# Side work of the mixers emitted by an account of engine times instead of at fixed distances

## The chip, the cores and the metric

One core of one Trainium2 chip runs the whole program. The metric is the device time of that core in microseconds (us), the median of several runs. Five instruction streams matter: TensorE (PE, matrix multiplications and transposes), VectorE (DVE), ScalarE (ACT), GpSimd (POOL) and SyncE (SP, which issues the DMAs). Each engine runs its own instructions in the order in which the program lists them; an instruction whose operand is not there holds back everything behind it on its engine.

## The reference, cut to what matters

Two layers run over 1024 prompt positions and 8 samples of 4 positions, 1056 columns in all, of width 1024.

```python
def _trunk(x, ...):
    for layer in range(DEPTH):                 # 2 layers
        h = _rmsnorm(x, p['norm_mix'][layer])
        if layer % 2 == 0:
            y, ... = _ab_mixer(h, ...)         # S5 scan + retention, 4 heads
        else:
            y, st = _hgrn_mixer(h, ...)        # gated recurrence, 8 heads
        x = x + y
        h = _rmsnorm(x, p['norm_ffn'][layer])
        y, buf = _conv_ffn(h, ...)             # gate, conv, silu, up, down
        x = x + y
    return _rmsnorm(x, p['norm_final']), ...
```

A mixer is a dense projection (`h @ w_in`), a recurrence over positions for each head, a norm of each head's output, a gate, and a dense projection back. All is in float32.

## The kernel before

**Dense work.** Every dense projection is cut into tiles of 128 output rows, and each tile into three column chunks of 384, 384 and 288 (`CH`). A float32 product is made of three reduced-precision ones (`mm1`: high with high, high with low, low with high), so a chunk of a mixer tile is 8 x 3 = 24 matmuls on line 258, into one of four PSUM buffers `acc`. After a chunk, `evac` moves it out, mostly with a DVE instruction (line 673 for the S5 input, 1032 to 1034 for rotated q and k, 1046 for v, 1460 for the q of layer 1).

**Jobs and ticks.** `run_jobs` (line 221 on) takes the tiles in a fixed list. After each k step `mm` advances a clock, `self.now`, by 1/8, so one chunk is one **tick** and one tile is three. `at(dt, fn)` files a piece of side work under a due time in ticks; `tick` runs what is due, and what runs is placed at that point in the program order of every engine that it uses. `chain` files a series of steps with given distances. All distances are constants in the table `P`. Nothing looks at whether the operands of a due step will be there: if not, PE, being in order, stands still. `flush` runs all that is left.

**Layer 0** (`layer0`, line 418 on). Input tiles u0 to u3, then for each of 4 heads the tiles q, k and v, then four gate tiles; before the last gate tile, `open2` flushes. Side work: the S5 scan, as `s5_x` (per unit u of 8, two pairs: `pair` builds operands on DVE and POOL, `turn` transposes on PE at line 856, `prod` multiplies at line 865), then `s5_within` (28 calls of five DVE instructions, lines 880 to 884), `s5_samples`, `s5_carry` (15 calls of the same five), then `s5_y` (per unit two pairs: spread, `toep` at line 971, `prod` at line 987). Beside it the retention of each head: `first(n)` (score and transpose, lines 1145 and 1146; `kt` copied by ACT at line 1150) and `second(n)` (lines 1161 to 1164; the state `S` is updated by DVE at line 1169), eight times, a sample chain `sample0` to `sample3`, and `head_norm` (line 1212 on).

**Layer 1** (`layer1`, line 1407 on). For each of 8 heads the tiles q, f and v; from the sixth head on a gate tile follows each head (`LAG` = 5), so the first five heads are 9 ticks long and the others 12. Side work is filed by `hgrn` at the end of the f tile: for each of three chunks `prep`, `scans` (1566, 1567), `base` (1578 to 1584), `level` three times (1601 to 1609) and `kfin` (1613); eight times `first(nn)` (1652, 1653, `levels` 1636, a masked DVE copy of the scores at 1657, `kt` copied by ACT at 1659) and `second(nn)` (1670 to 1673, the state `S` at 1676 or 1678 by DVE); the sample chain; and `head_norm`: `square`, `mean` (line 334, on `nl` made by POOL at line 325), `newton`, and `scale` (line 1235), once for each chunk.

With the constants of `P` (span 9, so u = 0.75 ticks), counted from the start of a nine-tick head: `first(n)` is due at 9.8 + 0.75 n, `second(n)` 1.05 later, the last step of the sample chain at 17.0, the head norm begins at 17.1, its three `mean` steps are due at 18.1, 18.5 and 18.8 and the first `scale` at 19.7. The q tile of the head after next begins at tick 18.

Of the kernel before, what the change touches and what calls it, by code (L numbers as in the profile page):

```python
# [11 lines left out]
F32R = mybir.dt.float32r  # L12
# [31 lines left out]
P = {"uP": 25, "qrV": 4, "loA": 3, "spV": 2, "wi": 0, "en2": 0, "stats": 1.281, "prep": 0.508, "fin": 0.8, "n1A": 1.101, "n1C": 1.0, "n2A": 0.386, "n2C": 0.45, "n3A": 0.501, "n3C": 0.375, "n4A": 0.558, "n4C": 0.78, "nsA": 0.429, "nsC": 0.339,   # L44
# [31 lines left out]

class Trunk:
    def __init__(self, ctx, tc, I, O):
        self.tc, self.nc, self.I, self.O = tc, tc.nc, I, O
        nc = self.core = self.nc  # L80
# [5 lines left out]
        self.uid = 0  # L86
        self.held = set()
# [106 lines left out]
    def at(self, dt, fn):  # L194
        self.seq += 1
        self.side.append(((self.now if self.base is None else self.base) + dt, self.seq, fn))
        self.side.sort(key=lambda x: x[:2])
# [5 lines left out]
    def put(self, dst, src, dt=None):  # L203

        self.at(P["put"] if dt is None else dt, lambda: self.nc.sync.dma_start(dst, src))

    def chain(self, t, steps):
        for dt, fn in steps:
            t += dt
            self.at(t, fn)  # L210
# [3 lines left out]

    def run_side(self, until):
        while self.side and (until is None or self.side[0][0] <= until):
            self.base, _, fn = self.side.pop(0)
            fn()
        self.base = None
# [137 lines left out]
    def prep_chunk(self, k, src, c0, c1, hx, wname, eng=None):  # L357
# [7 lines left out]
        if k == KD - 1 and eng is None:  # L365
            self.at(P["stats"], lambda: self.stats_done(c0, c1))
# [51 lines left out]
    def layer0(self):  # L418
# [7 lines left out]
        def start():  # L426
            self.ph = "A"
            self.lo_eng = [nc.gpsimd if P["loA"] & b else nc.vector for b in (1, 2)]
# [6 lines left out]
        def first():  # L435
# [67 lines left out]
            def finish():  # L503
# [12 lines left out]
                self.at(1.5, lambda: nc.sync.dma_start(self.st[:, :SEQ], self.I["rot"][1]))  # L516
                self.hold("powers")
                self.hold("rot")
                more = self.recorded(self.s5_setup2)
# [5 lines left out]
                for i in range(0, len(rot), 4):  # L525
                    self.at(P["rot"] + 0.04 * i, lambda i=i: [f() for f in rot[i:i + 4]])
# [9 lines left out]
        def u_work(rt):  # L536
# [5 lines left out]
            for j in range(1, 8):  # L542
                self.at(t + P["w"] * j, lambda j=j: self.s5_within(8 * rt, 8, j))
# [3 lines left out]
            self.at(t, self.s5_samples)  # L547
            for b in range(1, 16):
                self.at(t + P["ca"] * b, lambda b=b: self.s5_carry(b))
# [10 lines left out]
        self.job(lambda w: u_job(w, 3), I["w_ab"][3])  # L560
        for h in range(RH):
            R = {}
# [43 lines left out]
        for h in range(RH):  # L606
            if h == RH - 1:
                self.job(open2)
            self.job(lambda w, h=h: self.gate_tile(w, hx, yret[h], ys.get(4 + h)), I["w_ab"][16 + h])
# [185 lines left out]
    def u_load(self, u):  # L795
        nc = self.nc
        t = self.s5.tile([128, 4, 144], F32, tag="ush", name=self.nm("ush"), bufs=2)
# [8 lines left out]
    def bc(self, u):  # L806
        t = self.s5.tile([128, 4, 4, SH], F32, tag="bc", name=self.nm("bc"), bufs=2)
# [19 lines left out]
    def s5_x(self, u, t, dt, x1, x2):  # L827
# [3 lines left out]
        def pair(p):  # L831
# [16 lines left out]
            self.at(x1, lambda: turn(p, va))  # L848

        def turn(p, va):  # L850
# [7 lines left out]
            self.at(x2, lambda: prod(p, vt))  # L858

        def prod(p, vt):  # L860
            G = slice(4 * u + 2 * p, 4 * u + 2 * p + 2)
# [9 lines left out]
        self.at(t - 1.0, lambda: ld.update(bc=self.bc(u)))  # L871
        for p in range(2):
            self.at(t + p * dt, lambda p=p: pair(p))
# [61 lines left out]
    def s5_y(self, u, t, dt):  # L935
# [3 lines left out]
        def pair(p):  # L939
# [23 lines left out]
            self.at(P["y1"], lambda: toep(p, bz3, t3, ca3))  # L963

        def toep(p, bz3, t3, ca3):
# [11 lines left out]
            self.at(P["y2"], lambda: prod(p, ca3, t3))  # L977

        def prod(p, ca3, t3):
# [10 lines left out]
            self.free(("zb", p))  # L990
            for i in range(2):
# [6 lines left out]
        self.at(t - 1.0, lambda: ld.update(bc=self.bc(u)))  # L998
        for p in range(2):
            self.at(t + p * dt, lambda p=p: pair(p))  # L1000
# [20 lines left out]
    def rot_tile(self, w, hx, R, name, eng):  # L1021
# [4 lines left out]
        def evac(ci, ps, c0, c1):  # L1026
            n = c1 - c0
            t = self.tmp("rt")
            assert "rot" not in self.held
# [7 lines left out]
    def v_tile(self, w, hx, R):  # L1037
        nc = self.nc
        vt = self.hp.tile([128, 8, 128], F32, tag="vt", name=self.nm("vt"))
# [3 lines left out]
        def evac(ci, ps, c0, c1):  # L1043
# [3 lines left out]
            self.at(P["vt" + self.ph], lambda: tok(t, c0, c1))  # L1047

        def tok(t, c0, c1):
# [4 lines left out]
            if c1 > SEQ:  # L1054
                nc.tensor.transpose(pt[0:NS, 128 * nb:128 * nb + 128], t[:, 128 * nb:128 * nb + NS], self.ident)
                nc.scalar.activation(vs, pt[0:NS, 128 * nb:128 * nb + 128], AF.Copy)
                self.sample_v(pt[0:NS, 128 * nb:128 * nb + 128])
            b0 = c0 // 128
            nc.scalar.activation(vt[:, b0:b0 + nb].rearrange("p b e -> p (b e)"), pt[:, :128 * nb], AF.Copy)
        self.dense(w, hx, evac)  # L1060
# [67 lines left out]
    def retention(self, h, R, yret, span):  # L1128
# [4 lines left out]
        gam = 1.0 - 2.0 ** (-5.0 - h)  # L1133
        dq = self.hp.tile([128, 2, 128], F32, tag="dq", name=self.nm("dq"), bufs=1)
# [7 lines left out]
        def first(n):  # L1142
# [12 lines left out]
            st[n] = sT, kt, qd  # L1155

        def second(n):
            sT, kt, qd = st.pop(n)
            S = R["S"]
# [11 lines left out]
            R["S"] = S2  # L1171
            if n == SEQ // 128 - 1:
# [30 lines left out]
        lag = P["lagL"] if h == RH - 1 else P["lagA"]  # L1203
        for n in range(SEQ // 128):
            self.at(P["r0"] + u * n, lambda n=n: first(n))
            self.at(P["r0"] + u * n + lag, lambda n=n: second(n))
        t = P["r0"] + P["rs"] * u
        self.chain(t, [(0.0, sample0), (0.0, sample1), (lag, sample2), (P["kv" + self.ph], lambda: sample3(1))])
# [672 lines left out]
```

## Time and profile before

| | us |
|---|---|
| median of 3 runs | 2785.49 (2784.01 to 2785.78) |
| the profiled execution, run time | 2786.47 |
| its span, first to last instruction | 2784.5 |

A window row gives, for a stretch of the span, the busy time of each engine with the number of its instructions, then the mean granted clock of TensorE as a share of full speed (the clock has two levels, 1.2 and 2.4 GHz, so 0.50 and 1.00), then DMA. A wait row says which line of an engine waited for which instruction of another, in total, how often, and the longest one. A timeline row gives start, duration, engine, line, operation, what is written from what, and in brackets how long the engine had been idle and what ended that. Starts of different engines stand on one time axis.

### The profile page before, as it was taken

What the parts mean: (1) busy time and instruction counts of PE and PEld (TensorE: products, weight loads), DVE (VectorE), ACT (ScalarE), POOL (GpSimd) and SP (SyncE); (2) the same over time, 40 slices, a digit from 0 to 9 for tenths busy, and PEclk for the clock granted to TensorE, in tenths of its full rate; (3) what the DMA queues carried; (4) which work ended last, traced back from release to release, by engine and by line L of the source; (5) the groups of instructions that cost most, each with busy time, mean ns of one, the idle gap of its engine ahead of it and who ended that gap; (6) DMA issues with size and microseconds to landing.
All of it is one profiled execution on the core that took longest, in us unless ns stands there. A gap on an engine that the chain in (4) does not pass through costs nothing.

```text
span 2784.5 us, 42698 instructions
## 1 busy us (share of the span) xinstructions
PE 2632.7 (95%) x16388; PEld 2598.3 (93%) x16388; DVE 1623.1 (58%) x3414; ACT 978.2 (35%) x2120; POOL 780.9 (28%) x1173
## 2 busy tenths in 40 slices
PE   6778998999999999999989999989999999999998
PEld 5768998999999999999988889989999999999998
DVE  8996664565444444445787787765455444444445
ACT  4224444452212121214444445444432222222224
POOL 5636671321101010102434344442211010101013
PEclk8899999999999999999999999999999999999999
DMA  3412224111111111112211111112211111111112
GB/s 120 99 42 64 67 78 136 42 49 46 50 42 50 42 50 42 50 42 76 76 50 47 40 56 47 47 40 77 78 48 46 46 46 46 46 46 46 46 46 88
DMA packets 110539, 159.96 MB, mean 57 GB/s; under 512 B 18944, under 2 KB 48256, under 8 KB 110336
## 3 DMA queue, kind: packets, MB, share of 16 engines
q1 hardware_dynamic: 109760, 156.65, 17.9%
q8 instruction: 129, 2.11, 0.3%
q14 instruction: 74, 0.61, 0.1%
q10 hardware_dynamic: 576, 0.59, 0.1%
HBM read 136.45 MB, written 20.74 MB: 56 GB/s over the span
## 4 chain that ended last, share of the span: by engine, by line
PE 77%; DVE 15%; ACT 3%; issue 2%; POOL 1%; DMA 1%; SPq 1%; DVEq 0%; ACTq 0%; POOLq 0%
PE acc L258 71%; DVE hF L1606 1%; DVE s_t L881 1%; PE misc L1113 1%; DVE s_t L880 1%; DVE s_t L882 1%; DVE rb L351 1%; PE misc L1673 1%; DVE hS L1607 1%; DVE sall L884 0%; DVE lv L1601 0%; DVE sall L883 0%; DVE nsq L355 0%; DVE hR L1580 0%; DMA x<-in_x_dram 0%
## 5 line engine op out<-in xcount | busy, mean ns | idle before, releaser
L258 PE MATMUL acc<-hh,whi 128*128 128x384 f32 (+1 forms) x3320 | 1111.4, 335 | 9.2 <-ACT hh L284 7.0
L258 PE MATMUL acc<-hl,whi 128*128 128x384 f32 (+1 forms) x3320 | 1085.2, 327 | 8.8 <-DVE hl L290 8.8
L258 PE MATMUL acc<-hh,wlo 128*128 128x384 f32 (+1 forms) x3320 | 1084.4, 327 | 0.4 <-POOL wlo L189 0.4
L258 PEld LDWEIGHTS acc<-hl,whi 128*128 128x128 f32 x3320 | 635.8, 192 | 13.6 <-DVE hl L290 11.8
L258 PEld LDWEIGHTS acc<-hh,whi 128*128 128x128 f32 x3320 | 636.7, 192 | 11.0 <-ACT hh L284 7.8
L258 PEld LDWEIGHTS acc<-hh,wlo 128*128 128x128 f32 x3320 | 634.1, 191 | 1.0 <-POOL wlo L189 0.7
L1306 POOL TENSOR_TENSOR sl<-cv,rstd 128x384 f32<-128x384 f32 x132 | 122.0, 924 | 1218.4 <-ACT cv L345 1218.4
L188 ACT ACTIVATE whi<-raw 128x512 fp32r<-128x512 f32 x392 | 239.3, 620 | 394.1 <-PE acc L258 385.4
L189 DVE TENSOR_TENSOR wlo<-raw,whi 128x512 fp32r<-128x512 f32 x298 | 238.9, 802 | 143.9 <-ACT whi L188 141.1
L258 PE MATMUL acc<-hdl,whi 128*128 128x384 f32 (+1 forms) x984 | 318.2, 323 | 0.0
L258 PE MATMUL acc<-hdh,wlo 128*128 128x384 f32 (+1 forms) x984 | 318.2, 323 | 0.0
L258 PE MATMUL acc<-hdh,whi 128*128 128x384 f32 (+1 forms) x984 | 317.8, 323 | 0.0
L1335 DVE TENSOR_TENSOR x<-acc,x 128x384 f32<-128x384 f32 (+1 forms) x264 | 138.3, 524 | 239.4 <-PE acc L258 239.1
L258 PE MATMUL acc<-ys,whi 128*128 128x384 f32 (+1 forms) x768 | 187.8, 330 | 9.8 <-DVE x L617 3.7
L1298 ACT ACTIVATE cv<-ext,vec 128x384 f32<-128x384 f32 x132 | 90.6, 687 | 288.1 <-DVE ext L1286 226.8
L258 PEld LDWEIGHTS acc<-hdh,whi 128*128 128x128 f32 x984 | 185.1, 188 | 0.3
L258 PEld LDWEIGHTS acc<-hdl,whi 128*128 128x128 f32 x984 | 185.1, 188 | 0.3
L258 PEld LDWEIGHTS acc<-hdh,wlo 128*128 128x128 f32 x984 | 185.3, 188 | 0.0
L189 POOL TENSOR_TENSOR wlo<-raw,whi 128x512 fp32r<-128x512 f32 x94 | 127.5, 1358 | 203.7 <-ACT whi L188 202.9
L1300 DVE SCALAR_TENSOR_TENSOR cv<-ext,vec,cv 128x384 f32<-128x384 f32 x132 | 78.0, 591 | 169.2 <-ACT cv L1298 169.2
L282 ACT ACTIVATE hdh<-sl 128x384 fp32r<-128x384 f32 x132 | 65.9, 499 | 247.8 <-DVE sl L1323 247.8
L258 PEld LDWEIGHTS acc<-ys,whi 128*128 128x128 f32 x768 | 136.8, 192 | 12.8 <-DVE x L617 4.0
(379 smaller groups left out, 3636.6 us busy)
## 6 DMA issues: line engine op xcount, KB each, us to landing
raw<-in_w_gate_dram SPq DMA_DIRECT2D x88, 256.0 KB, 2.6
raw<-in_w_up_dram SPq DMA_DIRECT2D x88, 256.0 KB, 2.6
raw<-in_w_dn_dram SPq DMA_DIRECT2D x88, 256.0 KB, 2.6
raw<-in_w_c_dram SPq DMA_DIRECT2D x64, 256.0 KB, 2.7
raw<-in_w_ab_dram SPq DMA_DIRECT2D x40, 256.0 KB, 2.8
x<-in_x_dram SPq DMA_DIRECT2D x15, 528.0 KB, 7.2
ush<-uD SPq DMA_DIRECT2D x128, 34.0 KB, 1.9
xD<-x SPq DMA_DIRECT2D x8, 528.0 KB, 3.2
```

What stands on the lines that cost most here:

```text
L188: nc.scalar.activation(hi[:, s], raw, AF.Copy)
L189: eng.tensor_tensor(lo[:, s], raw, hi[:, s].bitcast(F32), OP.subtract)
L258: self.nc.tensor.matmul(ps[:, :c1 - c0], a[:, o:o + 128], b[:, c0:c1], start=first and p == 0, stop=last and p == 2)
L282: nc.scalar.activation(h, src, AF.Copy)
L351: self.nc.vector.scalar_tensor_tensor(b, b, -0.5, a, OP.mult, OP.mult)
L880: eng.tensor_tensor(t2[hi], s[lo], ms[lo].to_broadcast(half), OP.mult)
L881: eng.tensor_tensor(t2[lo], s[hi], ms[hi].to_broadcast(half), OP.mult)
L882: (eng2 or eng).tensor_tensor(t1, s, mr.to_broadcast(shape), OP.mult)
L1298: nc.scalar.activation(cv[:, :ln], ext[:, 0:ln], AF.Identity, bias=self.v(f"cb{l}", m), scale=cwv(0, m))
L1300: nc.vector.scalar_tensor_tensor(cv[:, :ln], ext[:, 1:ln + 1], cwv(1, m), cv[:, :ln], OP.mult, OP.add)
L1306: nc.gpsimd.tensor_tensor(s[:, :npr], cv[:, :npr], self.rstd[:, c0:c0 + npr], OP.mult)
L1335: nc.vector.tensor_tensor(X[m][:, c0:c1], ps, X[m][:, c0:c1], OP.add)
```

## The change

The constants in `P` stay as they are, and two are added. Three things are new.

An **account**. All five engines are wrapped, so that every instruction that the program emits is also entered into `Ahead`: one time per engine, plus times at which each operand was written and read. Prices are linear in the size, by engine. It keeps tiles by their names and so does not see that a buffer is reused. Reads of one tile by two engines are not ordered by it, and loads of ACT's function tables are not priced.

A **condition on each step**. `at` takes `need` (operands), `ok` (a test) and `thr` (a thread, in which a held step also holds those behind it). A step that is due runs only if `ok` holds and if the account says that its operands are ready within 100 ns (`slack`) of PE's own account; else it is held and looked at again at the next tick. A due time is thus a lower bound. A step of a chain is filed when the one before it has run.

**Requirements**. Where the program must go on, `require` runs filed steps in order of due time, whatever their `need` and due time, until a test holds. The q tile of layer 1 requires that the head before the last has its first `scale` behind it; so do the v tiles; gate and rotated tiles have requirements of their own. `flush` too goes by `ok` alone.

```diff
+class Ahead:
+    PER = {"vector": (75.0, 1.045, 70.0), "scalar": (110.0, 0.9, 60.0), "gpsimd": (150.0, 2.2, 60.0)}
+    def ready(self, *aps, eng="tensor"):      # latest end of a write of these operands
 ...
+    def call(self, eng, op, a, k):
+        out, ins = aps[0], aps[1:]
+        big = max(x.free_size() for x in aps)
+        t = max([self.at[eng], self.free(out, eng)] + [self.ready(x, eng=eng) for x in ins])
 ...
+            base, per, tail = self.PER[eng]
+            d = base + big * self.SLOW.get(op, per)
 ...
+            self.at[eng] = t + d
+            e = t + d + tail + 40.0
 ...
-    def at(self, dt, fn):
+    def at(self, dt, fn, need=None, ok=None, thr=None):
 ...
     def chain(self, t, steps):
-        for dt, fn in steps:
-            t += dt
-            self.at(t, fn)
+        def go():
+            fn()
+            if len(steps) > 1:
+                self.chain(0.0, steps[1:], **k)
+        self.at(t + dt, go, need, ok, **k)
 ...
+    def step(self, until):
+        barred = set()
+        for i, x in enumerate(self.side):
+            t, _, fn, need, ok, thr, _ = x
+            if until is not None and t > until:
+                return False
+            if thr in barred or (ok is not None and not ok()) or (
+                    until is not None and need is not None
+                    and self.when(need()) > self.ahead.at["tensor"] + P["slack"]):
+                if thr is not None:
+                    barred.add(thr)
+                x[6] = True
+                continue
+            self.side.pop(i)
+            self.base = max(t, self.now) if x[6] else t
+            fn()
 ...
+    def require(self, done):
+        while not done():
+            assert self.step(None)
 ...
@@ s5_x
-            self.at(x1, lambda: turn(p, va))
+            self.npair += 1
+            self.at(x1, lambda: turn(p, va), lambda: [va[:, :256]], lambda: p or self.nut < 2, "turn")
 ...
-            self.at(t + p * dt, lambda p=p: pair(p))
+            self.at(t + p * dt, lambda p=p: pair(p), None, lambda: "bc" in ld and self.npair < 3, "xpair")
 ...
@@ s5_y, pair
+                    lambda: "bc" in ld and self.cdone == 15 and ("zb", p) not in self.held, "ypair")
 ...
@@ samples (both mixers)
+        self.at(t, lambda: (begin(), self.chain(0.0, [
+            (0.0, one, of1, lambda: ...),
+            (lag, s2, lambda: of2() + of3(0)),
+            (P["kv" + self.ph], last, lambda: of3(1))], thr=key + "c")), ok=lambda: self.nsmp == 0 and self.stored("sst"), thr=key)
 ...
@@ head_norm
+            steps = [(P["ns" + self.ph] * ci, square), (P["n1" + self.ph], mean, lambda ci=ci: st[ci][1]),
 ...
@@ layer1, qtile
+            self.qheads.append(R)
+            self.require(lambda: len(self.qheads) < 3 or self.qheads[-3].get("normed"))
 ...
@@ hgrn
-            self.at(t0 + u * n, lambda n=n: first(n))
-            self.at(t0 + u * n + lag, lambda n=n: second(n))
+            self.at(t0 + u * n, lambda n=n: first(n), lambda n=n: of_first(n), lambda n=n: room(n), "rec1")
+            self.at(t0 + u * n + lag, lambda n=n: second(n), lambda n=n: of_second(n),
+                    lambda n=n: n in st and n in R.get("vt_in", ()), "rec2")
+        self.at(max(t0 + 7 * u + lag, t + lag + P["kv" + self.ph]) + 0.1, close, ok=over)
```

`of_second` lists `kt`, the scores `sT`, v, the decayed q and the state `S`; `room` asks that fewer than two `first` are pending; `over` that all eight `second` and the sample chain are done. The retention of layer 0 and the stores get conditions of the same kind.

## Rows read from the trace of the kernel before

**Rows 1.** The profile's page, part 1: busy time, share of the span, instructions.

```profile
PE 2632.7 (95%) x16388; PEld 2598.3 (93%) x16388; DVE 1623.1 (58%) x3414; ACT 978.2 (35%) x2120; POOL 780.9 (28%) x1173
```

**Rows 2.** Windows; columns stand in their first line: dense stretch, layer 0, layer 1.

```profile
core 0: us, PE busy (x) PEld busy (x) DVE busy (x) ACT busy (x) POOL busy (x), PEclk, DMA share, GB/s
700.00:1230.00 530.00, 530.00 (x3296) 530.00 (x3295) 238.03 (x425) 124.67 (x226) 68.93 (x150) 1.00 0.14 46
60.00:226.00 166.00, 117.68 (x679) 111.84 (x677) 156.09 (x454) 36.73 (x91) 81.49 (x140) 0.89 0.26 64
226.00:428.00 202.00, 187.73 (x1281) 184.00 (x1282) 128.26 (x306) 99.87 (x260) 135.32 (x220) 0.97 0.26 71
1430.00:1669.00 239.00, 212.28 (x1376) 206.39 (x1376) 190.81 (x447) 115.49 (x327) 97.42 (x93) 0.93 0.14 46
1669.00:1872.00 203.00, 182.58 (x1182) 178.27 (x1181) 142.23 (x334) 99.91 (x266) 87.05 (x84) 0.96 0.14 46
```

**Rows 3.** Waits of PE in 60 to 226: total us, times, longest.

```profile
PE misc L856 <- POOL va L847: 25.8, 6, 10.1
```

**Rows 4.** Waits of PE in 1430 to 1669.

```profile
PE misc L1670 <- ACT kt L1659: 14.9, 8, 2.4
PE misc L1673 <- DVE S L1676: 11.8, 4, 3.2
```

**Rows 5.** Waits of PE in 1669 to 1872.

```profile
PE misc L1670 <- ACT kt L1659: 12.4, 3, 4.6
```

**Rows 6.** DVE by line, 100 to 226: the costliest of five alike (880-884).

```profile
L881 DVE TENSOR_TENSOR s_t<-sall,ms 64x128 f32<-64x128 f32 (+1 forms) x43 | 20.3, 471 | 0.6
```

**Rows 7.** Timeline of PE: the first turn; the last toep and prod of S5.

```profile
70.62 0.69 PE L856 MATMUL misc<-ident,va 128*128 128x128 f32 x2 [10.09 <-POOL va L847]
...
421.34 0.39 PE L971 MATMUL misc<-ca,bz 128*128 128x128 f32 x2
426.87 0.39 PE L987 MATMUL misc<-sall,ca 128*128 128x136 f32 x2
```

**Rows 8.** Timeline of PE, a q tile of layer 1 from its first matmul.

```profile
1430.22 0.34 PE L258 MATMUL acc<-hh,whi 128*128 128x384 f32 x1
1434.63 0.38 PE L1053 MATMUL misc<-ident,vf 128*128 128x128 f32 x2
1435.88 0.29 PE L334 MATMUL misc<-nl,ones_h 128*128 128x288 f32 x1
1442.05 0.49 PE L1670 MATMUL misc<-vt,kt 128*128 128x128 f32 x2 [1.35 <-ACT kt L1659]
1448.42 0.80 PE L1670 MATMUL misc<-vt,kt 128*128 128x128 f32 x2 [2.37 <-ACT kt L1659]
1452.35 0.80 PE L1673 MATMUL misc<-hR,S 128*128 128x128 f32 x2 [2.71 <-DVE S L1676]
```

**Rows 9.** Timeline of DVE, same place.

```profile
1433.14 0.45 DVE L1046 TENSOR_TENSOR vf<-acc,rstd 128x288 f32<-128x288 f32 x1
1447.76 0.29 DVE L1657 COPY_PREDICATED sTb<-mdiag,misc 128x128 f32<-128x128 uint8 x1
1449.32 1.03 DVE L1235 SCALAR_TENSOR_TENSOR hy<-hy,vec,nsq 128x384 f32<-128x384 f32 x1
1452.01 0.28 DVE L1676 COPY S<-misc 128x128 f32<-128x128 f32 x1
```

**Rows 10.** Timeline of ACT, same place.

```profile
1432.26 1.28 ACT L336 ACT_TABLE_LOAD   x1
1433.56 0.58 ACT L338 ACTIVATE nsq<-misc,eps 128x384 f32<-128x384 f32 x1
1448.09 0.28 ACT L1659 ACTIVATE kt<-misc 128x128 f32<-128x128 f32 x1 [4.04 <-DVE sTb L1657]
```

**Rows 11.** Timeline of POOL, same place.

```profile
1434.07 1.44 POOL L325 TENSOR_TENSOR nl<-nsq,nh 128x288 fp32r<-128x288 f32 x1
```

More of the change, by code (lines that the diff above doesn't have):

```diff
@@ L203, in put, with stored, chain, go @@
     def put(self, dst, src, dt=None):
-        self.at(P["put"] if dt is None else dt, lambda: self.nc.sync.dma_start(dst, src))
-    def chain(self, t, steps):
-        for dt, fn in steps:
-            t += dt
-            self.at(t, fn)
+        name = self.ahead.place(src)[0]
+        self.out[name] = self.out.get(name, 0) + 1
+        def go():
+            self.nc.sync.dma_start(dst, src)
+            self.out[name] -= 1
+            if not self.out[name]:
+                del self.out[name]
+        self.at(P["put"] if dt is None else dt, go, lambda: [src])
+    def stored(self, s):
+        return not any(n.startswith(s + "_") for n in self.out)
+    def chain(self, t, steps, **k):
+        dt, fn, *more = steps[0]
+        need, ok = (more + [None, None])[:2]
+        def go():
+            fn()
+            if len(steps) > 1:
+                self.chain(0.0, steps[1:], **k)
+        self.at(t + dt, go, need, ok, **k)
     def flush(self):
         self.run_side(None)
-    def run_side(self, until):
[L216 to L219, printed above, removed]
+    def step(self, until):
[14 more added lines that the diff above has]
+            fn()
+            self.base = None
+            return True
+        return False
+    def when(self, need):
+        return need if isinstance(need, float) else self.ahead.ready(*need)
+    def run_side(self, until):
+        while self.step(until):
+            pass
+        assert until is not None or not self.side, [x[5] for x in self.side]
+    def require(self, done):
+        while not done():
+            assert self.step(None)
     def run_jobs(self):
@@ L542, in u_work @@
             for j in range(1, 8):
-                self.at(t + P["w"] * j, lambda j=j: self.s5_within(8 * rt, 8, j))
+                self.at(t + P["w"] * j, lambda j=j: self.s5_within(8 * rt, 8, j), None,
+                        lambda: "powers" not in self.held and self.xdone >= 4 * (rt + 1), "within")
             if rt < 3:
@@ L1028, in evac @@
             t = self.tmp("rt")
[L1029 removed]
+            self.require(lambda: "rot" not in self.held)
             nc.scalar.activation(t[0:64, :n], ps[64:128], AF.Copy)
@@ L1714, in hgrn, with room @@
+        def room(nn):
+            new = {0: 2, 1: 0, 2: 1}[nn % 3]
+            return self.pend < 2 and nn // 3 in R["fin"] and all(("sTb", (self.nst + x) % 3) not in self.held for x in range(new))
         for ci in range(3):
-            self.at(P["h0"] + 3 * u * ci, lambda ci=ci: prep(ci))
+            self.at(P["h0"] + 3 * u * ci, lambda ci=ci: prep(ci), None,
+                    lambda ci=ci: ("f0", ci == 2) not in self.held and self.nlive < P["live"], "prep")
         for n in range(SEQ // 128):
-            self.at(t0 + u * n, lambda n=n: first(n))
```

220 lines of the change are left out of this document (188 added, 32 removed).

## The prediction

> **What bounds the kernel now.** I read the busy shares first, then windows, then the waits of PE in the windows that lose time, then one such place in the timelines of all engines. PE is busy 95% of the span [rows 1], so a gain can come only from its idle time and from time at the lower clock. In the dense stretch neither exists: 530 us of 530 busy, granted clock 1.00, 3296 matmuls, so 160.8 ns each, and a tick of 24 is 3.86 us. In the mixers both exist [rows 2]. A stretch's idle time is its length less PE's busy time; what the clock costs is (1 less the mean granted clock) times the length, as the clock is either at 2.4 or at 1.2 GHz:
>
> - layer 0, 60 to 226: 48.3 idle + 0.11 x 166 = 18.3 by the clock, 66.6 us;
> - layer 0, 226 to 428: 14.3 + 0.03 x 202 = 6.1, 20.4 us;
> - layer 1, 1430 to 1669 (four nine-tick heads): 26.7 + 0.07 x 239 = 16.7, 43.4 us, or 10.9 for each head;
> - layer 1, 1669 to 1872: 20.4 + 0.04 x 203 = 8.1, 28.5 us.
>
> That is 158.9 us, 5.7% of the span, and the most that the change can reach. The waits are the kind that it aims at: side matmuls emitted before their operands were there, `turn` before its POOL operand in layer 0 [rows 3], `second` before `kt` or the state `S` in layer 1 [rows 4, 5]. What came last is a queue, mostly DVE's. At 1442 to 1452 PE stands three times within ten us, 1.35 + 2.37 + 2.71 [rows 8], and the last time the state copy starts at 1452.01 on DVE [rows 9], though its matmul was done by 1442.5: it lay behind some 9 us of levels and norms.
>
> **The change part by part.** No arithmetic, DMA or tile is added or removed. Instructions are moved, and since due times stay as lower bounds, a step can move only to a later tick, unless a requirement pulls it forward. The account itself runs while the program is built and costs the chip nothing.
>
> *Layer 0, 60 to 226.* Held here: `turn` and `prod` of the S5 input, and what follows through `ok` (at most three pairs in flight, where the fixed distances, a pair each 0.74 ticks and 3.0 from `pair` to `prod`, gave four; then `s5_within`, `s5_carry`). The first `turn` alone costs 10.09 us of PE [rows 7]. But DVE is busy 156.1 of these 166 us [rows 2]. Its work up to the end of the carry is the same after the change: 43 calls of five instructions take about 5 x 19 us of it (the costliest line 20.3 [rows 6]), and each dense tile needs its evacuation from the same queue. If PE runs ahead, it stops at the four PSUM buffers instead of at `turn`. `s5_y` cannot begin before its due tick, which falls at the end of this stretch, so the same ticks and the same DVE work lie before it. The gain is bounded by DVE's idle time, 9.9 us, and from below by 0; I take 6, nearer to the bound, because the stalls are what spaces DVE's work. What is late next: DVE.
>
> *Layer 0, 226 to 428.* DVE is busy 128 of 202 us and POOL 135 [rows 2], so there is cover for held steps: the dense q, k, v and gate chunks. Of the 20.4 us I take back 12; bounds 0 and 20.4. Behind held PE steps there queue only their own chain and thread. The price: the last `prod` of S5 is due about 0.2 ticks before the flush ahead of the last gate tile, so any delay of the S5 chain puts steps into the flush, where nothing covers them. One pair's way from `toep` to `prod` is 5.5 us now (421.34 to 426.87 [rows 7]); I charge 3, with bounds 0 (it catches up) and 11 (both pairs).
>
> *Layer 1, 1430 to 1669.* For the heads whose `second` is held, the three stalls above fall away, and with them the low clock, except where the account promises too early. Two such places show. `kt` is copied by ACT only when the masked copy on DVE is through (1447.76 + 0.29, then 1448.09 [rows 9, 10]), which the account doesn't order, and it knows no table load, 1.28 us on ACT each time [rows 10]. So I leave the first stall, 1.35 us, standing.
> Against this stands the new requirement. At the start of a q tile (1430.22 [rows 8]) the first `scale` of the head before the last must be emitted; before, it ran at 1449 [rows 9], as it is due at tick 19.7 of its head and the q tile begins at 18. So at four q tiles everything due within 1.7 ticks is emitted at once, ahead of the tile, without asking for operands: three `mean`, one transposition of v, two `first`, and on DVE a `base`, two `level` and the newton steps. In the order of due times the transposition (operand ready at 1433.14 + 0.45 on DVE [rows 9]) and the third `mean` (operand ready at 1434.07 + 1.44 = 1435.51 on POOL [rows 11]) hold PE, where before 18 dense matmuls lay between. The block's own matmuls are some 2 us, so PE idles about 1435.5 - 1430.2 - 2.0 = 3.3 us. With 1.35 left and about 1.5 for the clock (a third of the 4.2 per head that 6.7 us of stalls now cost), a head loses 6.1 in place of 10.9: 4.8 x 4 = 19 us gained. The bounds are 43.4 (nothing is left) and -28 (the rival below).
>
> *Layer 1, 1669 to 1872.* Twelve-tick heads; their first `scale` is due 2.6 ticks before the q tile that requires it, so nothing is forced. Longest stall 4.6 us, on `kt` [rows 5]. DVE is busy 142 of 203 [rows 2]. I take 60% of 28.5, 17 us, the same share as in layer 0 after 226; bounds 0 and 28.5.
>
> *Queues.* Weight fetches keep their places, except that two conversions come up to a tick early in the forced blocks. Stores wait for their source by the account and so stand less at the head of SP's queue; the waits of PE on weights or stores are too few to price: 0, and no loss while fetches lie a tile ahead.
>
> Sum: 6 + 12 - 3 + 19 + 17 = 51 us. The profiled execution took 2786.5, 1 us above the median of the runs; 2786.5 - 51 = 2735.5, and **2735** against the median.
>
> **The rivals.**
>
> *The account promises too early, or DVE only hands the wait on.* If readiness is under-priced wherever DVE and ACT are congested, steps are released while `kt` or `S` is still queued, and PE stands as before. DVE is busy 191 of 239 us in layer 1 [rows 2]; with the stalls gone it would be at 191 of 196, so part must come back as waits for PSUM buffers. For it: the two unpriced things above. Against it: the long stalls are queueing behind DVE instructions that the account does add up. Then about a third of the gain stays: 2786 - 17 = 2769.
> The Trainium skill, page "PSUM — Partial Sum Buffer", section "PSUM bank collisions raise a hardware error", says that two engines must not access one bank and quadrant at once, reads included, so their reads have to be ordered; by that rule all 64 `kt` copies wait for the masked copy, and the trace agrees at 1448.09 [rows 10].
> If each of the 64 were released just when the account says, with about 0.3 us (the masked copy's 0.29 [rows 9]) still to come, 64 x 0.3 = 19 us would go back to PE; this is within this rival.
>
> *The forced blocks grow: slower than before.* The sample chain ends at tick 17.0 and the norm begins at 17.1, one tick before the q tile. If holding delays either by about a tick (3.9 us of dense work), the whole norm and two `second` of the next head fall into the block, without `need`. PE then stands through DVE's queue, from 1435.9 to the state copy at 1452.3, less 3 us of work: 13 us, and 5 by the clock, 18 per head in place of 10.9, 4 x 7 = +28. With 11 for an uncovered S5 tail, and only 6 + 17 regained elsewhere: 2786 + 28 + 11 - 23 = 2802. For it: DVE's queue of 9 us is longer than the margin. Against it: no wait stands on the sample chain now, and the held `second` have six more to catch up in.
>
> *Nearly all comes back.* The holds are exact, the blocks find their operands ready: 9.9 + 18 + 35 + 25 = 88 us, 2698. Against it: DVE would have to run at over 95% without making anybody wait.
>
> *The change does nothing* would need that the account never holds a step. With 10 us between `turn` and its operand that can't be; no chance of its own.
>
> **How the numbers follow.** Forecast 2735, own range 2712 to 2757: 0.48. Too early or handed on, 2757 to 2783: 0.25. Forced blocks, 2783 to 2815: 0.15. Nearly all, 2685 to 2712: 0.12. The range 2698 to 2792 leaves out about half of the last case and most of the upper half of the third, some 0.17. A measurement of this kernel can tell about 0.2% from no change, 5.6 us: faster is below 2779.9, same up to 2791.1. Faster: 0.48 + 0.12 + 0.19 of the second case = 0.79; same: 0.06 + 0.04 = 0.10; slower 0.11.
>
> **What would show it.** Right: the waits of line 1670 on `kt` and of 1673 on `S` under 10 us together between 1430 and 1669 (26.7 now), the wait of line 856 on `va` gone, the granted clock there above 0.96, and at four q tiles a new wait of lines 1053 and 334, 2 to 4 us each. DVE's share in 60 to 226 above 95%, with the carry ending no more than 10 us earlier than now. Wrong: waits of line 258 on line 673, 1032 or 1460, PE halted by full PSUM buffers (the second case); waits of 1670 and 1673 right at a q tile's start over 10 us (the third); S5 matmuls emitted after the last gate tile's flush with waits ahead of them; or the end of layer 0 moved by more than 25 us, which would mean that DVE was no bound there.

## The result and the profile after

The changed kernel takes 2847.16 us (median of 4 runs, 2844.68 to 2848.75) against 2785.64 (4 runs, 2784.01 to 2786.56): a ratio of 1.0221, 95% interval 1.0203 to 1.0238. It is slower by 61.5 us; 2735 was forecast. The profiled execution's span is 2842.9 us, and the page's first part, beside [rows 1], shows that PE's work hardly grew while its share fell:

```profile
PE 2652.2 (93%) x16388; PEld 2611.0 (92%) x16388; DVE 1610.9 (57%) x3414; ACT 983.2 (35%) x2126; POOL 778.8 (27%) x1173
```

All instructions now go through one wrapper and stand under line L171, so the views of after are read by tile names. To find the place, I take the first dense matmul of each tile from the timelines of both kernels (us; in brackets the time since the row above):

| from the start of | before | after |
|---|---|---|
| q tile of head 2, layer 0 | 233.8 | 210.6 |
| k tile of head 2 | 254.3 (20.5) | 269.0 (58.4) |
| third gate tile | 410.5 (156.2) | 421.3 (152.3) |
| last gate tile, behind the flush | 428.2 (17.7) | 492.6 (71.3) |
| FFN, layer 0 | 569.8 (141.6) | 633.4 (140.8) |
| first q tile, layer 1 | 1339.6 (769.7) | 1403.2 (769.8) |
| output tiles, layer 1 | 1907.5 (568.0) | 1962.9 (559.7) |

Layer 1's mixer gains 8.3 us. Layer 0's loses 63.6, in two places: the q tile of head 2, and the flush ahead of the last gate tile. Where the first of them begins, the changed kernel is still 23 us *ahead*.

Windows of after, with the columns of [rows 2], for the same two stretches of layer 0 and for the flush, then the whole mixer of layer 0 to the start of its FFN, in before and in after:

```profile
60.00:226.00 166.00, 130.07 (x777) 126.37 (x777) 119.94 (x343) 43.21 (x108) 81.33 (x138) 0.88 0.28 72
226.00:428.00 202.00, 146.10 (x950) 141.27 (x949) 119.78 (x322) 77.50 (x187) 105.54 (x162) 0.86 0.18 52
428.00:520.00 92.00, 67.18 (x353) 62.53 (x353) 45.12 (x112) 34.14 (x78) 32.56 (x64) 0.74 0.36 104
```

```profile
60.00:570.00 510.00, 439.31 (x2754) 427.71 (x2753) 358.29 (x881) 203.15 (x467) 252.77 (x394) 0.94 0.26 74
```

```profile
60.00:633.00 573.00, 453.11 (x2743) 438.95 (x2743) 346.67 (x880) 209.82 (x472) 250.20 (x393) 0.87 0.23 66
```

The first row is the surprise: DVE, 156.1 us busy there before [rows 2], is busy 119.9. PE does more dense work, DVE less of its own. What is missing is the S5 chain. Windows of the tile `s_t` alone (all five DVE instructions of a `within`, `carry` or `s5_samples` call and of an output spread on DVE write or read it; 28 x 5 + 15 x 5 = 215 of before's 250 are `within` and `carry`) in before, then in after:

```profile
core 0: us, DVE busy (x), PEclk, DMA share, GB/s
60.00:226.00 166.00, 93.48 (x225) 0.89 0.26 64
226.00:300.00 74.00, 12.99 (x25) 0.93 0.27 76
```

```profile
60.00:226.00 166.00, 43.23 (x107) 0.88 0.28 72
226.00:300.00 74.00, 33.98 (x124) 0.66 0.09 26
```

Half of it now comes later, and all at once. Timelines of after at that place, DVE, then ACT, then PE (columns as in [rows 7]):

```profile
225.45 0.81 DVE L171 TENSOR_TENSOR s_t<-sall,ms 64x128 f32<-64x128 f32 x2
...
241.18 0.43 DVE L171 TENSOR_TENSOR s_t<-sall,ms 64x32 f32<-64x32 f32 x2
...
257.02 0.46 DVE L171 TENSOR_TENSOR sall<-sall,s_t 128x32 f32<-128x32 f32 x2
...
265.25 0.28 DVE L171 TENSOR_TENSOR sT<-misc,dq 128x128 f32<-128x128 f32 x1
```

```profile
224.84 0.38 ACT L171 ACTIVATE sall<-misc 128x256 f32<-128x256 f32 x1
265.63 0.37 ACT L171 ACTIVATE kt<-misc,cst 128x128 f32<-128x128 f32 x1 [40.41 <-DVE sT L171]
```

```profile
229.01 0.29 PE L171 MATMUL acc<-hh,wlo 128*128 128x288 f32 x1
266.05 0.80 PE L171 MATMUL misc<-qr,qr 128*128 128x128 f32 x2 [36.74 <-ACT kt L171]
```

With the last `prod` of the S5 input run, the last seven `within` calls (225.45 on), the samples, all fifteen `carry` calls (241.18 to 257.5) and the first two output pairs pass their tests together, their due times long gone, and so enter DVE's queue back to back: 40 us of it. Behind them stands the `sT` of a retention step (265.25), behind that `kt` on ACT, and PE, which needs the buffers that these release, stands 36.74 us. PE stands for 10.5 and 9.5 us at two earlier batches of seven calls as well (from 148.8 and 187.3 on). The view names no releaser for these two; the batches hold DVE from 142.3 to 157.5 and from 181.6 to 196.0, and PE goes on at 159.2 and 196.8.

The flush is the other place. Waits of PE in 428 to 510, and the last of them in PE's timeline:

```profile
PE misc L171 <- DVE bz L171: 13.4, 3, 9.5
PE misc L171 <- DVE S L171: 5.5, 1, 5.5
```

```profile
485.72 2.04 PE L171 MATMUL misc<-ca,bz 128*128 128x128 f32 x8 [3.40 <-DVE bz L171]
```

Before, the last `toep` ran at 421.34 [rows 7]. In after the first runs at 282 (230 before) and the last at 488; seven of the sixteen lie behind the start of the third gate tile (one in before), so the S5 output finishes with little dense work beside it.

In layer 1, four nine-tick heads (start of the second v tile to the start of the first gate tile) took 255.9 us and now take 255.4. Waits of PE in 1490 to 1725, to set beside [rows 4], and two q tiles' forced blocks in PE's timeline:

```profile
PE misc L171 <- ACT kt L171: 9.5, 2, 4.9
PE misc L171 <- DVE vf L171: 7.4, 4, 2.4
PE misc L171 <- DVE S L171: 4.3, 2, 2.2
```

```profile
1495.62 0.90 PE L171 MATMUL misc<-ident,vf 128*128 128x128 f32 x3 [2.37 <-DVE vf L171]
...
1553.10 0.55 PE L171 MATMUL misc<-ident,vf 128*128 128x128 f32 x3 [1.35 <-DVE vf L171]
1555.98 0.49 PE L171 MATMUL misc<-qm,km 128*128 128x128 f32 x2 [0.59 <-ACT rb L171]
1561.47 0.80 PE L171 MATMUL misc<-vt,kt 128*128 128x128 f32 x2 [4.89 <-ACT kt L171]
```

The 26.7 us of waits on `kt` and `S` became 13.8, plus 7.4 on `vf` in the blocks that the requirement forces ahead of the q tiles. What the holds and what the blocks do here is taken apart below.

### The profile page after: what moved, and what is told of

Read it like the earlier page. It is cut to its first block, busy times and chain, and to the rows that moved or that the text cites. A ratio compares the mean times of both kernels' runs of the same rounds, so it can differ in the third digit from the quotient of the medians.

```text
span 2842.9 us, 42664 instructions
## 1 busy us (share of the span) xinstructions
PE 2652.2 (93%) x16388; PEld 2611.0 (92%) x16388; DVE 1610.9 (57%) x3414; ACT 983.2 (35%) x2126; POOL 778.8 (27%) x1173
## 4 chain that ended last, share of the span: by engine, by line
PE 77%; DVE 14%; ACT 3%; issue 3%; POOL 1%; SPq 1%; DMA 1%; DVEq 0%; POOLq 0%; ACTq 0%
PE acc L171 71%; PE misc L171 6%; DVE s_t L171 2%; DVE hR L171 1%; DVE sall L171 1%; DVE hF L171 1%; DVE lv L171 1%; SPq L171 1%; DVE hS L171 1%; DVE rb L171 1%; ACT sTb L171 1%; DVE set L171 0%; DVE hl L171 0%; DVE ba L171 0%; DVE sst L171 0%
## 5 line engine op out<-in xcount | busy, mean ns | idle before, releaser
L171 PE MATMUL acc<-hh,whi 128*128 128x384 f32 (+1 forms) x3320 | 1100.2, 331 | 14.2 <-ACT hh L171 6.7
L171 PE MATMUL acc<-hl,whi 128*128 128x384 f32 (+1 forms) x3320 | 1082.6, 326 | 8.1 <-DVE hl L171 8.1
L171 PE MATMUL acc<-hh,wlo 128*128 128x384 f32 (+1 forms) x3320 | 1081.3, 326 | 6.1 <-POOL wlo L171 5.7
L171 PEld LDWEIGHTS acc<-hh,whi 128*128 128x128 f32 x3320 | 632.4, 191 | 16.6 <-ACT hh L171 7.5
L171 PEld LDWEIGHTS acc<-hl,whi 128*128 128x128 f32 x3320 | 632.0, 190 | 12.6 <-DVE hl L171 11.3
L171 PEld LDWEIGHTS acc<-hh,wlo 128*128 128x128 f32 x3320 | 630.9, 190 | 9.7 <-POOL wlo L171 8.4
L171 POOL TENSOR_TENSOR sl<-cv,rstd 128x384 f32<-128x384 f32 (+2 forms) x176 | 150.9, 868 | 1218.9 <-ACT cv L171 1218.9
L171 ACT ACTIVATE whi<-raw 128x512 fp32r<-128x512 f32 x392 | 239.3, 621 | 421.6 <-PE acc L171 385.3
L171 DVE TENSOR_TENSOR x<-acc,x 128x384 f32<-128x384 f32 (+1 forms) x360 | 187.6, 522 | 280.3 <-PE acc L171 280.0
L171 DVE TENSOR_TENSOR wlo<-raw,whi 128x512 fp32r<-128x512 f32 x298 | 238.7, 801 | 145.5 <-ACT whi L171 142.7
L171 PE MATMUL acc<-hdl,whi 128*128 128x384 f32 (+1 forms) x984 | 317.9, 323 | 0.0
L171 PE MATMUL acc<-hdh,wlo 128*128 128x384 f32 (+1 forms) x984 | 317.7, 323 | 0.0
L171 PE MATMUL acc<-hdh,whi 128*128 128x384 f32 (+1 forms) x984 | 317.3, 322 | 0.0
L171 DVE SCALAR_TENSOR_TENSOR cv<-ext,vec,cv 128x384 f32<-128x384 f32 (+1 forms) x264 | 156.1, 591 | 173.6 <-ACT cv L171 168.9
L171 PE MATMUL acc<-ys,whi 128*128 128x384 f32 (+1 forms) x768 | 188.8, 331 | 9.7 <-DVE x L171 2.9
L171 POOL TENSOR_TENSOR wlo<-raw,whi 128x512 fp32r<-128x512 f32 x98 | 134.4, 1374 | 220.5 <-ACT whi L171 213.1
L171 ACT ACTIVATE cv<-ext,vec 128x384 f32<-128x384 f32 x132 | 90.6, 686 | 288.4 <-DVE ext L171 226.9
L171 PEld LDWEIGHTS acc<-hdl,whi 128*128 128x128 f32 x984 | 184.9, 188 | 0.3
L171 PEld LDWEIGHTS acc<-hdh,whi 128*128 128x128 f32 x984 | 184.8, 188 | 0.3
L171 PEld LDWEIGHTS acc<-hdh,wlo 128*128 128x128 f32 x984 | 185.1, 188 | 0.0
L171 ACT ACTIVATE hdh<-sl 128x384 fp32r<-128x384 f32 x132 | 65.8, 499 | 247.8 <-DVE sl L171 247.8
L171 PEld LDWEIGHTS acc<-ys,whi 128*128 128x128 f32 x768 | 137.5, 193 | 12.9 <-DVE ys L171 3.6
```

What stands on the lines that cost most here:

```text
L171: return fn(*a, **k)
```

## The experiments

The letters of the theories are explained in each text. Times without an interval are single runs beside a run of the kernel before on the same chip (2785.16 for e1 to e4, 2784.59 for e5 to e10). "Layer 0 ends" means the first matmul of its output projection, 439.8 us in before and 504.3 in after.

### In which layer

e3 drops operands, tests and threads in layer 0, e4 in layer 1; requirements stay in both.

```diff
 def at(self, dt, fn, need=None, ok=None, thr=None):
+    if self.ph == "A":        # e3; "C" in e4
+        need = ok = thr = None
```

> While layer 0 is emitted, no step has conditions, so its order is that of fixed distances; layer 1 keeps the account and the requirements. If the whole loss is layer 0's and layer 1 has gained what its stage times say (568.0 to 559.7 us), the time is 2786 - 8 = 2778, within 3. If the layers depend on each other through what is left over between them, it lies elsewhere.

> The reverse: conditions in layer 0 alone, layer 1 in the order of fixed distances. By the same reading 2847 + 8 = 2855, within 3, with layer 0 ending at 504 us as in the changed kernel.

e3 took 2780.04 us: layer 0 ends at 438.6, layer 1's mixer takes 559.6. e4 took 2848.78: layer 0 ends at 506.4. The whole loss is layer 0's. Layer 1's conditions and requirements are worth 8.4 us in its mixer, of which its output projection and norm give 2.8 back (96.2 us in before, 99.0 in e3). e4 lies 6 us below its expectation, which took all 8 us to be the conditions' and to last to the end: its layer 1 mixer takes 566.4, so the requirements alone are worth 1.6, and its output projection and norm take 95.5.

### Held by the account, or by the tests

e1 lets the account hold nothing, tests and threads stay. e2 keeps the account and allows five S5 pairs in flight in place of three. e7 does both.

```diff
-P = {"slack": 100.0, ...          # e1, e7
+P = {"slack": 1e9, ...
-... lambda: "bc" in ld and self.npair < 3, "xpair")      # e2, e7
+... lambda: "bc" in ld and self.npair < 5, "xpair")
```

> The margin of the account is 1e9 ns in place of 100, so no step is ever held for its operands; the tests (limits on how many pairs are in flight, buffers, order) and the requirements stay. Theory A (the tests slow the S5 input chain: three pairs in flight in place of four, and its successors then leave in one batch): layer 0 stays slow, the last input product later than 200 us, time above 2825 us. Theory B (the account's holds slow the chain): with them gone the chain is back near 164 us and the time is within 10 us of 2786.

> The limit on S5 input pairs in flight is five in place of three, all else as changed. Theory A: the last input product comes back from 222 us to below 185, the batch of 22 DVE calls that stopped PE for 36.7 us is split, and the time falls by 30 us or more, to 2815 or less. Theory B: the chain stays late (above 205 us) and the time within 10 us of 2847.

> No step is held for its operands (as in e1_no_need, 2820 us), and in addition up to five S5 input pairs may be in flight in place of three. Theory A1 (of the tests it is this limit that slows the chain): the last input product back below 175 us from 197, time 2785 to 2795. Rival A2 (another test does, such as the one u tile or the order of bc loads): still above 2810.

Starts in us, from the timelines of PE:

| | total | last S5 input `prod` | first and last `toep` | layer 0 ends |
|---|---|---|---|---|
| before | 2785 | 164 | 230, 421 | 439.8 |
| e7, no account, five pairs | 2794.65 | 164 | 228, 432 | 451.4 |
| e1, no account, three pairs | 2820.11 | 197 | 249, 453 | 472.3 |
| e2, account, five pairs | 2834.83 | 195 | 249, 476 | 493.0 |
| after, account, three pairs | 2847.16 | 222 | 282, 488 | 504.3 |

Each of the two delays the S5 input chain by some 30 us alone, and together by 58; with the account the output chain from `toep` to `toep` is longer as well (227 us in e2, 204 in e1). The limit of three pairs costs 25 us without the account and 12 with it, the account 27 to 40 by the same four times. So neither alone is the cause: e1 and e2 each fell between their theories A and B, and e7 came out as A1. With both gone the input chain is where it was, and so is DVE's work in its stretch, 156.09 us as in before [rows 2]; e7's windows of 60 to 226:

```profile
60.00:226.00 166.00, 120.28 (x677) 114.87 (x678) 156.09 (x457) 37.38 (x93) 82.13 (x141) 0.87 0.27 65
```

The 10 us that e7 still loses come in the output chain (204 us from `toep` to `toep`, 191 in before); which of the remaining tests makes them was not taken apart. Layer 0 ends 16 to 20 us behind the last `toep` in all five: S5's chain sets its end.

### Which steps

e9 frees only the S5 steps and the stores of layer 0 from the conditions; e10 is the mirror: in layer 0 only S5 steps have them.

```diff
+    s5 = any(n in fn.__qualname__ for n in (".s5_", ".u_work.", ".put."))
+    if self.ph == "A" and s5:       # e10: and not s5, without ".put."
+        need = ok = thr = None
```

> The changed kernel, but in layer 0 the steps of the S5 scan (input pairs, within, samples, carry, output pairs) and the stores go at their fixed distances as before; retention, norms and splits of layer 0 keep operands, tests and threads, layer 1 is as in the changed kernel. Theory A (the loss of layer 0 is the held S5 chain: its steps come late and then in batches): layer 0 ends within 8 us of the kernel before (output projection at 432 to 448 us), last input product at 160 to 170, total 2772 to 2788. Theory G (the holding of the retention steps also feeds the batches, as they are what DVE's queue holds beside the scan): layer 0 ends at 455 us or later, total above 2800.

> The mirror of the run before: in layer 0 only the S5 steps have operands, tests and threads; retention, norms, splits and stores go at fixed distances; layer 1 as in the changed kernel. Theory A: nearly the whole loss stays, layer 0 ends at 490 to 510 us, total 2835 to 2855. Theory G: at most half of it, layer 0 ends before 472 us, total below 2820.

e9 took 2777.37 us, e10 2831.78. Layer 0 ends at 434.9 and at 490.5. Windows of 60 to 226 in e9, then in e10:

```profile
60.00:226.00 166.00, 117.92 (x676) 111.38 (x675) 155.03 (x455) 36.73 (x91) 82.07 (x140) 0.89 0.26 64
```

```profile
60.00:226.00 166.00, 119.53 (x718) 116.23 (x716) 123.13 (x358) 38.19 (x96) 77.14 (x134) 0.84 0.27 69
```

DVE is back at 155 us with S5 at fixed distances, and at 123 with only S5 held. Holding S5 steps loses 50.7 of the 64.5 us; holding the retention's steps gains 4.9 (7.5 in the second profile of the same kernel, e9_timed, so it is known to a few us only). (e10 fell short of the bounds set for theory A, by 3 us in the total.) Why the two together lose 14 us more than S5's holds alone was not taken apart.

### The batches by themselves

e6 is the kernel before, with the seven `within` calls of a tile due at one time, and the fifteen `carry` calls too. e5 is the changed kernel with both filed one after another at the old distances once the first may go.

```diff
-                self.at(t + P["w"] * j, ...s5_within(8 * rt, 8, j))                 # e6
+                self.at(t + P["w"] * 7 + 0.001 * j, ...s5_within(8 * rt, 8, j))
-                self.at(t + P["ca"] * b, ...s5_carry(b))
+                self.at(t + P["ca"] * 15 - 0.001 * (15 - b), ...s5_carry(b))
```

```diff
+            def carry(b):                                                          # e5; within alike
+                self.s5_carry(b)
+                if b < 15:
+                    self.at(P["ca"], lambda: carry(b + 1), None, okc, "carry")
 ...
```

> The kernel before, with one edit in layer 0: the seven DVE calls of each S5 block are due all at the time of the last of them, and so are the 15 calls of the carry; nothing else moves and nothing is held. Theory C (what stops PE is the batch itself: some 14 us of DVE work, and 16 us and more for the carry, put into DVE's in-order queue at one place): new waits of PE of 5 to 15 us at each batch, and 2785 + 20 to 50 us. Rival D (batches are harmless, it is the lateness of the chain that costs): within 8 us of 2785.

> The changed kernel, but the seven DVE calls of each S5 block and the 15 of the carry are each filed when the one before has run, at the distances of the kernel before, so that a late chain can't release them in one batch. Theory C: the waits of 10.5, 9.5 and 36.7 us in 146 to 266 us go, layer 0 reaches its tile k2 some 30 us earlier (269 us now), though S5's output part starts later and more of it falls into the flush: time 2815 to 2840. Rival D: the lateness alone costs; the time stays at 2847 or above.

e6 took 2808.49 us, 23.9 more than before, and layer 0 ends 22 us later, as theory C had it. The last due time of each batch is the old one, and nothing else differs. Its waits of PE from 140 to 260, where before has none over 4.5 us:

```profile
PE misc L1145 <- ACT kt L1150: 13.9, 1, 13.9
PE misc L1161 <- ACT kt L1150: 11.8, 1, 11.8
PE misc L1053 <- DVE vf L1046: 9.5, 1, 9.5
PE misc L856 <- DVE s_xs L869: 8.3, 1, 8.3
```

e5 took 2822.66, 24.5 less than after, inside theory C's range. What stays is lateness: its dense tiles run ahead of before up to the third gate tile (397.0 against 410.5), but the first `toep` comes at 291, and from the third gate tile to the last it takes 76.6 us (17.7 in before), with this wait of PE, 425 to 490:

```profile
PE misc L171 <- DVE bz L171: 18.3, 6, 6.7
```

So the batches cost some 24 us by both runs, and the lateness the other 37 or so, in the flush.

### The forced blocks of layer 1

e8 is e3 with a third buffer for the q tiles, so that the norm is required one head later. e12 is e9 with a requirement that runs only steps of the head norm while there are any, in place of everything due before them.

```diff
-            self.require(lambda: len(self.qheads) < 3 or self.qheads[-3].get("normed"))     # e8
-            q = self.hp.tile([128, NT], F32, tag="kr", name=self.nm("hq"))
+            self.require(lambda: len(self.qheads) < 4 or self.qheads[-4].get("normed"))
+            q = self.hp.tile([128, NT], F32, tag="kr", name=self.nm("hq"), bufs=3)
```

```diff
         while not done():                                                                   # e12
-            assert self.step(None)
+            x = next((x for x in self.side if self.ph == "C" and ".head_norm." in x[2].__qualname__
+                      and (x[4] is None or x[4]())), None)
+ ...                        # run x; without one, self.step(None)
```

> Layer 1 alone by the account (as in e3_layer1_only, 2780 us), with three buffers for its q tiles in place of two, so that a q tile requires the norm of the head three before and forces nothing. Theory E (the forced blocks at four q tiles eat what the holds give back): the extra of 6 and 11 us that the tiles before q2 to q5 now take falls away, stalls of second stay held, time 2755 to 2770. Rival F (layer 1 is bound by DVE, and the blocks only show where): within 5 us of 2780.

> The version with the S5 steps and the stores of layer 0 at fixed distances and everything else as in the changed kernel, once more, timed against the kernel before: 2777 to 2778 us if the look at it holds (layer 0 5 us shorter, layer 1 2 to 3 us shorter than before), a ratio of 0.9973 to 0.9976. If both were accidents of one execution, 2783 to 2788.

> The version before it, and in layer 1 a requirement runs only the steps of the head norm that it needs, not everything else that is due before them (the transposition of v, two first halves, base, two levels), so the forced block ahead of the q tiles no longer waits for v or for the transposed keys. Theory E (the block's content is what costs): the waits of 2.4 us on v and 4.9 us on the transposed keys at four q tiles go, and their 12 to 18 us with them: 2760 to 2767. Theory F (DVE's queue is the bound there, as the run with a third q buffer suggests: waits gone at the q tile come back on weights converted late and on the transposed keys): 2774 to 2784, with new waits of dense matmuls in the f and v tiles of 1 to 4 us each.

e8 took 2786.45 us, 6.4 more than e3 and outside both theories' ranges. The waits on `vf` and the long ones on `kt` are gone, but in the v tiles dense matmuls now wait for their own weights. The wait row of PE in 1430 to 1669 (columns as in [rows 4]), the timeline of ACT at one of the four places, and that of PE:

```profile
PE acc L171 <- ACT whi L171: 13.3, 4, 3.9
```

```profile
1515.22 0.62 ACT L171 ACTIVATE whi<-raw 128x512 fp32r<-128x512 f32 x1
1521.46 1.28 ACT L171 ACT_TABLE_LOAD   x1 [5.63 <-DVE hz L171]
1522.76 0.52 ACT L171 ACTIVATE hz<-hz 128x384 f32<-128x384 f32 x1
1523.19 0.61 ACT L171 ACTIVATE whi<-raw 128x512 fp32r<-128x512 f32 x1
```

```profile
1523.85 0.69 PE L171 MATMUL acc<-hh,whi 128*128 128x384 f32 x1 [3.88 <-ACT whi L171]
```

The weights' conversion stands on ACT behind the sigmoid of `hz`, which waits 5.63 us for DVE: by my reading, the norm, put off by a head's time, now meets the levels and the evacuations in DVE's queue. Theory E fell: taking the forced block away hands the wait on. Of the 6.6 us that its layer 1 mixer takes more than e3's, 1.9 lie in the four nine-tick heads (255.5 and 253.5) and 5.1 in the last gate tile (18.1 and 12.9).

e4 is the other half, the requirements without layer 1's conditions: there these heads take 253.8 us. Its waits of PE in 1490 to 1725:

```profile
PE misc L171 <- DVE S L171: 12.6, 4, 3.7
PE misc L171 <- DVE vf L171: 9.5, 4, 2.4
```

The blocks' waits on `vf` are there, and those on `kt` are gone though nothing is held. So against the 255.9 us of before neither the forced blocks without holds (e4) nor the holds without a block at the q tile (e8) change these heads by more than 2.1 us, and both together give 255.4 (after) and 253.5 (e3).

The e9 kernel again, timed: 2776.73 us (8 runs) against 2785.79 (12 runs), ratio 0.9972 (0.9962 to 0.9983). e12: 2769.23 (5 runs), ratio 0.9943 (0.9930 to 0.9955). Its layer 1 mixer takes 550.3 us (559.9 in e9). The same four heads, in before and in e12, and PE's waits in e12 there:

```profile
1413.00:1669.00 256.00, 229.28 (x1492) 222.96 (x1491) 203.77 (x476) 122.66 (x344) 104.09 (x99) 0.93 0.14 47
```

```profile
1409.00:1656.00 247.00, 228.72 (x1489) 217.63 (x1489) 202.16 (x475) 120.92 (x344) 109.27 (x99) 0.98 0.15 49
```

```profile
PE misc L171 <- DVE S L171: 5.3, 8, 1.1
PE misc L171 <- ACT kt L171: 4.8, 8, 1.3
```

The result lies between theories E and F: 7.5 us gained, the waits on `vf` gone and the longest on `kt`, 4.6 us in e9, cut to 1.3. So with the holds in place, what the block carries costs, and not that the norm is required. e12 is the version that beats both kernels.

## Why the prediction was wrong

**What bounds the kernel.** That the time to be had is PE's idle time in the mixers was right. The account of it was too large: the clock was counted on idle time too. A stretch is its busy plus its idle time, and the low clock can lengthen only the first. In layer 0 the 63 us are 49.2 more idle (70.7 to 119.9) and 13.8 more busy; the formula of the prediction gives 0.13 x 573 - 0.06 x 510 = 43.9 for the clock alone. In e12's four heads the clock went from 0.93 to 0.98, which the formula prices at 13.0 us (0.07 x 256 - 0.02 x 247); busy time fell by 0.6, idle time by 8.4.

**Layer 0, 60 to 226: +6 with a floor of 0. This is the step that failed.** "The same ticks and the same DVE work lie before it" was taken from the due times, but a due time is only a floor: where a chain is held, its DVE work moves past the stretch. 107 of 225 `s_t` instructions remained in it. The dense tiles did run ahead, by 23.2 us at the q tile of head 2, past the upper bound of 9.9, and all of that and more was paid behind. The other half of the step was wrong too: DVE's 156 of 166 us were read as a bound that would stay. In before it was one, for DVE waited only 1.2 us there for other engines. In after it stood idle for 46 us. The largest of its waits in 60 to 226:

```profile
DVE s_xs L171 <- ACT sall L171: 11.9, 11, 2.8
DVE qr L171 <- ACT rt L171: 10.2, 6, 2.5
```

So the scan did not stand behind a full queue; its steps had been placed later in the program, or stood behind one whose operand was late (`s_xs` is the copy behind a `prod`). What holds them is shown: S5's holds alone take DVE's share away (e9, e10), and without the account's holds and with five pairs it is back (e7). By my reading PE's stall before `turn`, 25.8 us [rows 3], was the price for a scan at full pace, because a PE that stands still runs no dense chunk while DVE goes on with the scan. That evacuations of dense chunks got ahead of the scan is at most a part: `qr`, and `vf` with 5.9 us more, make 16.1 of the 46 us. The prediction named the limit of three pairs and gave it no price; e1 and e7 put it at 25 us, e2 and after at 12.

**226 to 428: +12, and the flush: -3, bounds 0 to 11.** This is where the failed step was paid. From the q tile of head 2 to the last gate tile before took 194.4 us, after 282.0. The prediction had the right place ("any delay of the S5 chain puts steps into the flush"), but sized it as two pairs' way. Delay is not bounded by a pair: with the input chain 58 us late, seven of sixteen `toep` came after the third gate tile's start, and from there to the last gate tile it took 53.6 us longer. The batch that stops PE for 36.74 us at 229 was in no term: steps past their due time leave together, however far apart they were filed.

**Layer 1, 1430 to 1669: +19, measured +0.5.** The place was right: the v transposition and the norm, run at the q tile without asking. The size was not. A block was put at 3.3 us of idle time; half of them cost 2.37, the others 1.35 + 0.59 + 4.89 = 6.83, since a `second` whose `kt` has to come through DVE and ACT is forced with them. From the first matmul of a v tile to that of the q tile behind the block, the four took 103.9 us in place of 66.8, the q tiles behind them 56.2 in place of 99.5, and the f tiles 78.6 in place of 73.0. Nor was the gain of the holds there to be had as priced: without the block at the q tile (e8) these heads gain 0.5 us, as other waits come in place of those on `kt` and `S`. e12 shows that this part was to be had: with the block cut to the norm, the same four heads take 247.2 us, 255.3 in e9.

**1669 to 1872: +17, measured 7.7** (202.6 to 194.9 us from the first gate tile to the sixth), with the direction right: no block is forced there in front of the q tiles.

**The rivals.** The slower one put the cause in the forced blocks; with them layer 1 was still no slower than before. Its addition, an uncovered S5 tail of 11 us, was part of the true cause, at a fifth of the 53.6 us that the flush grew by. The measured 2847 lies beyond even this case's 2815, and for another reason than it gave. "Handed on" is what e8 shows in layer 1, with weights in place of PSUM buffers. "Too early": where it was to show, in layer 1, the waits on `kt` left in e12 are 4.8 us over the 32 `second` of four heads, 0.15 each, where 0.3 was priced. The Trainium skill, page "PSUM — Partial Sum Buffer", section "PSUM bank collisions raise a hardware error", asks that accesses of two engines to one bank and quadrant be ordered. The trace agrees in ACT's start behind DVE's copy (1448.09 [rows 10]). What PE then waits is decided by where the step is placed.

**What would show it.** Two of the signs named came: S5 matmuls in the flush with waits ahead of them, and an end of layer 0 moved by more than 25 us, "which would mean that DVE was no bound there". It moved by 64.5, to the other side. Of the signs of being right, the wait before `turn` on `va` fell from 25.8 to 4.6 us in 60 to 226 (the 10.5 us ahead of the `turn` at 159.23 stand beside a batch), and new waits of 1.35 to 2.37 us came at the four q tiles; but `kt` and `S` kept 13.8 us where under 10 was asked, the granted clock there stayed at 0.93 (1490 to 1725) where above 0.96 was asked, and DVE's share in 60 to 226 fell to 72%, where above 95% was asked.

## What to carry to other kernels

Where the dense stream is made to wait for a side chain, ask which of the two ends the stage: a stall that lets a long chain go at full pace is a price for its end time, and taking the stall away pays only if the chain has slack (e9 holds the short retention chains and gains 5 us, e10 holds the scan and loses 51). A condition that replaces a distance must keep the spacing as well, or everything overdue leaves in one tick (24 us, e6); and a step that has to be forced should take only what it needs with it (7.5 us, e12).

## What was not expected of the hardware

A higher granted clock by itself was worth little: 0.93 to 0.98 over four heads of layer 1 (before and e12) came with 0.6 us less busy time of PE in 229. Idle time explains only a part of that: a mean of 0.93 over 256 us makes some 36 us at the lower of the two levels (0.07 x 256 / 0.5), and PE was idle for 26.7. Why its busy time did not fall by more stays open.
